# Strassen blocks of a gated up-projection: two taken together with interleaved products instead of one at a time, weight sums in buffers of their own, 19 activations kept in DRAM

## The chip, the core and the metric

The kernel runs on one core of a Trainium2 chip. The metric is the device time of one execution in microseconds, and the number to predict is the median of several executions of the changed kernel, against the median of the kernel before.

## The reference, cut to what matters

The whole program is one residual layer (a mixer and a feed-forward part). The change touches only the feed-forward part, which in numpy-like form is, for 512 tokens, model width D = 1024 and hidden width 2816:

```python
u, g = split(h @ w_ffn_up)             # h: 512 x 1024, w_ffn_up: 1024 x (2 x 2816)
g = causal_depthwise_conv3(g) + bias
act = gelu(g) * u                      # 512 x 2816
y = act @ w_ffn_down                   # 2816 x 1024, then scaled, residual, layer norm
```

All of it is fp32 in accuracy: each operand is held as a high part and a low part (fp32r), and a product is three matmuls (high x high, high x low, low x high).

## The kernel before

**Blocks.** The hidden width is cut into 22 blocks j of 128 columns. Each block has two units of weights of 128 x 1024: the gate unit 2j+1 and the value unit 2j. A plain block loads a unit (`wload`), casts it to its high part on ACT and subtracts on DVE for the low part (`wsplit`, L225 and L214), and runs 48 matmuls of 128 x 512 on PE (`up_mm`, lines L246 to L248). Its results stand in the PSUM tiles `acc` (gate, `gtile`) and `s` (value, `vtile`), two of each, taken by j mod 2. `gate_half` then copies, convolves (ACT L1203, then two DVE scalar_tensor_tensor, L206) and applies gelu (`gelu2`: ACT L566, DVE, ACT L568, DVE, a ping-pong between the two engines), and `val_half` multiplies by the value unit (DVE `tt`, L211).

**Fast blocks.** The blocks in `FAST` use Strassen's scheme (Winograd's form) on the 2 x 2 split of the two units and the tokens: seven products of 12 matmuls of 128 x 256 (`prod`, L1263) instead of eight. That needs four sums of weight halves on POOL (`gtt`, L349), each 128 x 512, and seven operand splits (`half`: an ACT cast L1226 and a DVE subtraction L214). The sums of the tokens (`x_combos`) are made once. In the order of its products, a fast block computes a (tile `hd`), copies a into b (`acc`, ACT L1283), computes c (`hd`) and copies it to SBUF (ACT L1286), adds a product to b, then forms d = b + c into `s` (DVE `tt`, L211) before b gets its next product. The sums are written over the halves they come from, in the `gab` tiles of the loaded units, so a sum waits for the split of the half that it overwrites. Six buffers hold split operands (`wh` and `wl` in turn, three of each).

**Order.** One block follows the other: 5, 7, 8, 10, 11, 13, 14, 16 and 17 are fast, the others plain; blocks 0 and 1 are computed ahead. Each engine's instructions run in the order in which a scheduler has put them, and the tile pools place the waits on buffers. After a block, `ada2_step` does parts of a modulation product on DVE (a scale of loaded weights, two scalar_tensor_tensor per part, tiles `s5h`), at the blocks listed in `MODS`. The first 8 activations (`NSP`) are written to DRAM and read back in the down-projection; the others are split at once and kept.

**Tail.** `tail_product` runs the down-projection over the 22 activations in the order `down`, three matmuls for each high and low pair, and prepares its weights (scale L211, cast L225, subtract L214) meanwhile.

Of the kernel before, what the change touches and what calls it, by code (L numbers as in the profile page):

```python
# [32 lines left out]
NF = 22  # L33
# [107 lines left out]
FAST = (5, 7, 8, 10, 11, 13, 14, 16, 17)  # L141
MODS = (6, 9, 12, 15, 18, 18, 19, 19)
NSP = 8
# [18 lines left out]
def _build(ctx, tc, nc, h):  # L162
# [1048 lines left out]
    def val_half(j, gg, ov):  # L1211
        if len(ov) == 1:
            tt(gg, ov[0], gg)
        else:
            for i in range(2):
                sl = slice(256 * i, 256 * i + 256)
                tt(gg[:, sl], ov[i][:, 0:256], gg[:, sl])
        if j < NSP:
            dma(spill[j * P:(j + 1) * P, :], gg)
            gp_.append(None)  # L1220
        else:
            gp_.append(pair_of(gg, "hb" if j < 14 else "s5b" if j < 15 else "hx" if j < 18 else "gab"))
# [7 lines left out]
    optag = iter(("wh", "wl") * (4 * NF))  # L1230
# [35 lines left out]
    def fast_pair(j):  # L1266
        wg_, wv_ = (wload(h["wup"][u], tag="gab") for u in (2 * j + 1, 2 * j))
        a11, a12, a21, a22 = wg_[:, :512], wg_[:, 512:], wv_[:, :512], wv_[:, 512:]
        b, d = gtile[j % 2], vtile[j % 2]
        a, c = bank("hd"), bank("hd")  # L1270
        w1 = half(a11)
        gtt(a21, a11, a21, ALU.subtract)
        s3 = half(a21)
        w4 = half(a22)
        gtt(a22, a22, a21, ALU.subtract)
        s2 = half(a22)
        w2 = half(a12)
        gtt(a11, a22, a11, ALU.add)
        s1 = half(a11)
        gtt(a12, a12, a22, ALU.subtract)  # L1280
        s4 = half(a12)
        prod(a, w1, xq(0, 0), True)
        A.copy(b[:, 0:256], a[:, 0:256])  # L1283
        prod(c, s3, xc(3), True)
        cs = hh(256)
        A.copy(cs, c[:, 0:256])  # L1286
        prod(b, s2, xc(2))
        tt(d[:, 0:256], b[:, 0:256], cs, ALU.add)
        prod(a, w2, xq(1, 0))
        prod(b, s1, xc(1))  # L1290
        v = hh(256)
        tt(v, b[:, 0:256], cs, ALU.add)
        prod(d, w4, xc(4))
        prod(b, s4, xq(1, 1))
        gg = gate_half(j, (a, b))
        val_half(j, gg, (d, v))
# [14 lines left out]
    for j in range(NF):  # L1311
        if j == G2J:
            g2 = grow(1, 0.5, "hd")
        if j >= FJ:
            first.append(scaled(h["wfd"][NSP + len(first)], g2, None))
        if j == NS // 2:
            x_combos()
        if j in FAST:
            fast_pair(j)
        else:  # L1320
# [23 lines left out]
    down = list(range(NSP, 18)) + list(range(NSP)) + list(range(18, NF))  # L1344
    got = {}

    def act_at(k):
        for kk in range(k, min(k + 3, NF)):
# [8 lines left out]
            got[kk] = pair_of(x, "s5h" if j < 4 else "hx" if j < 7 else "hb")  # L1357
# [20 lines left out]
```

## Time and profile before

| | |
|---|---|
| median of 3 runs (lowest, highest) | 897.4 us (896.97, 900.19) |
| the profiled execution | 899.05 us, span of its instructions 897.3 us |
| PE busy | 831.3 us, 93% of the span |
| DVE busy | 661.8 us, 74% |
| ACT busy | 389.7 us, 43% |
| POOL busy | 161.4 us, 18% |
| mean granted TensorE clock | 0.98 |

Busy shares are averages over a program with several stages. The change touches the stretch from 506.8 us, where the up-projection's block 2 begins, to the end. In the timeline rows below the first number is the start, the second the duration; several instructions that follow each other stand in one row with xN, and the bracket tells how long the engine was idle before and what released it.

### The profile page before, as it was taken

What the parts mean: (1) busy time and instruction counts of PE and PEld (TensorE: products, weight loads), DVE (VectorE), ACT (ScalarE), POOL (GpSimd) and SP (SyncE); (2) the same over time, 40 slices, a digit from 0 to 9 for tenths busy, and PEclk for the clock granted to TensorE, in tenths of its full rate; (3) what the DMA queues carried; (4) which work ended last, traced back from release to release, by engine and by line L of the source; (5) the groups of instructions that cost most, each with busy time, mean ns of one, the idle gap of its engine ahead of it and who ended that gap; (6) DMA issues with size and microseconds to landing.
All of it is one profiled execution on the core that took longest, in us unless ns stands there. A gap on an engine that the chain in (4) does not pass through costs nothing.

```text
span 897.3 us, 12212 instructions
## 1 busy us (share of the span) xinstructions
PE 831.3 (93%) x4430; PEld 685.5 (76%) x4430; DVE 661.8 (74%) x1232; ACT 389.7 (43%) x656; POOL 161.4 (18%) x285
## 2 busy tenths in 40 slices
PE   3999999999999999999999799977969799999996
PEld 1777878787777788888878688866868787888885
DVE  5557888788688855499888876868687688799044
ACT  4455464545656432333345544444445444345000
POOL 2771221112130000000024402414132200000000
PEclk9999999999999999999999899999889899999998
DMA  9832221312112344586550252332222053567011
GB/s 340 293 106 70 64 89 60 93 39 82 63 60 87 126 138 168 180 295 216 178 198 13 83 187 95 117 129 71 94 95 72 1 175 130 161 203 242 4 48 47
DMA packets 47725, 110.21 MB, mean 123 GB/s; under 512 B 13616, under 2 KB 14512, under 8 KB 47664
## 3 DMA queue, kind: packets, MB, share of 16 engines
q1 hardware_dynamic: 47664, 109.42, 36.9%
q8 instruction: 35, 0.57, 0.3%
q14 instruction: 26, 0.21, 0.1%
HBM read 103.11 MB, written 4.19 MB: 120 GB/s over the span
## 4 chain that ended last, share of the span: by engine, by line
PE 59%; DVE 21%; ACT 6%; DMA 4%; issue 4%; POOL 3%; SPq 2%; DVEq 0%; ACTq 0%; POOLq 0%
PE acc L246 8%; PE acc L248 8%; PE acc L247 8%; PE hd L246 6%; PE hd L247 6%; PE hd L248 6%; DVE hh L206 5%; DVE wl L214 3%; PE acc L1263 3%; POOL gab L349 3%; PE s L246 2%; PE s L248 2%; PE s L247 2%; SPq L196 2%; DVE wh L214 1%
## 5 line engine op out<-in xcount | busy, mean ns | idle before, releaser
L225 ACT CAST wh<-w 128x1024 fp32r<-128x1024 f32 (+2 forms) x85 | 84.5, 997 | 122.9 <-PE acc L247 73.2
L214 DVE TENSOR_TENSOR wl<-w,wh 128x1024 fp32r<-128x1024 f32 (+2 forms) x85 | 100.3, 1183 | 39.2 <-ACT wh L225 38.3
L246 PE MATMUL acc<-hp,wh 128*128 128x512 f32 x256 | 103.4, 405 | 0.4 <-ACT hx L789 0.4
L248 PE MATMUL acc<-hp,wl 128*128 128x512 f32 x256 | 102.0, 398 | 0.0
L247 PE MATMUL acc<-hp,wh 128*128 128x512 f32 x256 | 101.9, 398 | 0.0
L1028 POOL TENSOR_SCALAR mov<-mov 128x1 f32<-128x1 f32 x6 | 3.6, 608 | 326.6 <-ACT s L1027 160.2
L246 PEld LDWEIGHTS acc<-hp,wh 128*128 128x128 f32 x256 | 48.2, 189 | 14.7 <-issue 3.7
L248 PEld LDWEIGHTS acc<-hp,wl 128*128 128x128 f32 x256 | 48.2, 188 | 11.3 <-issue 0.4
L247 PEld LDWEIGHTS acc<-hp,wh 128*128 128x128 f32 x256 | 48.4, 189 | 10.8 <-issue 0.4
L349 POOL TENSOR_TENSOR gab<-gab,gab 128x512 f32<-128x512 f32 (+1 forms) x31 | 42.4, 1378 | 64.6 <-DMA gab<-in_wup 30.6
L206 DVE SCALAR_TENSOR_TENSOR s5h<-hh,k,s5h 128x512 f32<-128x512 f32 x56 | 41.7, 781 | 2.0 <-DMA hh<-in_wa 1.7
L1263 PE MATMUL acc<-hp,wl 128*128 128x256 f32 x120 | 21.5, 343 | 20.0 <-ACT acc L1283 19.8
L206 DVE SCALAR_TENSOR_TENSOR hh<-hd,hh 128x512 f32<-128x512 f32 (+3 forms) x40 | 24.4, 609 | 18.2 <-ACT hd L568 9.1
L1263 PEld LDWEIGHTS acc<-hp,wl 128*128 128x128 f32 x120 | 19.7, 248 | 21.0 <-ACT acc L1283 20.6
L214 DVE TENSOR_TENSOR wh<-gab,wh 128x512 fp32r<-128x512 f32 x32 | 26.5, 830 | 10.5 <-ACT wh L1226 10.5
L247 PE MATMUL hd<-s5b,wh 128*128 128x512 f32 (+1 forms) x88 | 32.2, 367 | 0.5 <-DVE s5b L214 0.5
L246 PE MATMUL hd<-s5b,wh 128*128 128x512 f32 (+1 forms) x88 | 31.8, 367 | 0.7 <-ACT s5b L1179 0.5
L225 ACT CAST hb<-hh 128x512 fp32r<-128x512 f32 (+3 forms) x44 | 24.7, 561 | 17.7 <-DVE hh L206 11.0
L248 PE MATMUL hd<-s5b,wl 128*128 128x512 f32 (+1 forms) x88 | 31.9, 364 | 0.0
L349 POOL TENSOR_TENSOR gab<-gab 128x512 f32<-128x512 f32 (+1 forms) x13 | 16.1, 1248 | 85.8 <-DVE wl L214 45.8
L1226 ACT CAST wh<-gab 128x512 fp32r<-128x512 f32 x32 | 19.4, 618 | 25.8 <-POOL gab L349 13.4
L214 DVE TENSOR_TENSOR wl<-gab,wl 128x512 fp32r<-128x512 f32 x31 | 28.5, 920 | 2.3 <-ACT wl L1226 1.5
(629 smaller groups left out, 2370.1 us busy)
## 6 DMA issues: line engine op xcount, KB each, us to landing
hh<-in_wa SPq DMA_DIRECT2D x64, 256.0 KB, 4.3
w<-in_win SPq DMA_DIRECT2D x30, 512.0 KB, 3.3
w<-in_wup SPq DMA_DIRECT2D x26, 512.0 KB, 3.4
w<-in_wfd SPq DMA_DIRECT2D x22, 512.0 KB, 3.7
gab<-in_wup SPq DMA_DIRECT2D x18, 512.0 KB, 3.4
hb<-in_wa SPq DMA_DIRECT2D x16, 512.0 KB, 7.3
w<-in_wglu SPq DMA_DIRECT2D x8, 512.0 KB, 3.4
w<-in_wdn SPq DMA_DIRECT2D x8, 512.0 KB, 3.3
```

The lines of the kernel that those rows point to most:

```text
L196: return nc.sync.dma_start(o, i)
L206: V.scalar_tensor_tensor(o, i0, s, i1, op0=op0, op1=op1)
L214: V.tensor_tensor(o, a, b, op=ALU.subtract)
L225: A.copy(hi, x)
L246: T.matmul(o, lhsT=wh, rhs=xh, start=first, stop=False)
L247: T.matmul(o, lhsT=wh, rhs=xl, start=False, stop=False)
L248: T.matmul(o, lhsT=wl, rhs=xh, start=False, stop=last)
L349: GP.tensor_tensor(o, a, b, op=op)
L1028: GP.tensor_scalar(v[:, 2:3], v[:, 0:1], v[:, 1:2], EPS * D, op0=ALU.add, op1=ALU.add)
L1226: A.copy(o[:, 0], src)
L1263: T.matmul(o[:, 0:256], lhsT=w[:, p, sl], rhs=x[k][y], start=first and k + i == 0, stop=k == 3 and i == 2, skip_group_check=True)
```

## The change

`FAST` now lists pairs: (5,6), (8,9), (11,12), (14,15) and (17,18), so ten blocks are fast and twelve plain. Between two pairs stands one plain block, and 19, 20 and 21 are plain at the end. `fast_pairs` emits the 14 products of a pair's blocks x and y in turns: a_x, c_x, a_y, c_y, b_x, a_x, b_y, a_y, b_x, d_x, b_y, d_y, b_x, b_y. The sums go into `hx` tiles of their own. Operands go to six `hb`, three `wh`, three `wl` and again two `hb` buffers. Two short buffers of a block become the halves of one `hh` tile. `x_combos` stands at block 4 in the source. Nineteen activations are written to DRAM and read back in the down-projection, which takes them in the order 0 to 21, and the parts of the modulation product are done at other blocks.

```diff
@@ -138,9 +138,10 @@
 MKR = 6
 PF = 1
 G2J = 20
-FAST = (5, 7, 8, 10, 11, 13, 14, 16, 17)
-MODS = (6, 9, 12, 15, 18, 18, 19, 19)
-NSP = 8
+FAST = (5, 8, 11, 14, 17)
+XJ = 4
+MODS = (7, 10, 10, 13, 13, 16, 16, 19)
+NSP = 19
 FJ = 21
 QUICK = (1, 3)
 LAST = ((0, 0, 512), (1, 0, 256), (1, 256, 512))
@@ -1219,7 +1220,7 @@
             dma(spill[j * P:(j + 1) * P, :], gg)
             gp_.append(None)
         else:
-            gp_.append(pair_of(gg, "hb" if j < 14 else "s5b" if j < 15 else "hx" if j < 18 else "gab"))
+            gp_.append(pair_of(gg, "gab"))
 
     def half(src):
         o = big((P, 2, 512), F32R, next(optag))
@@ -1227,7 +1228,7 @@
         sub(o[:, 1], src, f32(o[:, 0]))
         return o
 
-    optag = iter(("wh", "wl") * (4 * NF))
+    optag = iter((("hb",) * 6 + ("wh", "wl") * 3 + ("hb",) * 2) * NF)
     xd = []
 
     def x_combos():
@@ -1263,37 +1264,52 @@
                 T.matmul(o[:, 0:256], lhsT=w[:, p, sl], rhs=x[k][y], start=first and k + i == 0, stop=k == 3 and i == 2,
                          skip_group_check=True)
 
-    def fast_pair(j):
+    def fast_operands(j):
         wg_, wv_ = (wload(h["wup"][u], tag="gab") for u in (2 * j + 1, 2 * j))
         a11, a12, a21, a22 = wg_[:, :512], wg_[:, 512:], wv_[:, :512], wv_[:, 512:]
-        b, d = gtile[j % 2], vtile[j % 2]
-        a, c = bank("hd"), bank("hd")
-        w1 = half(a11)
-        gtt(a21, a11, a21, ALU.subtract)
-        s3 = half(a21)
-        w4 = half(a22)
-        gtt(a22, a22, a21, ALU.subtract)
-        s2 = half(a22)
-        w2 = half(a12)
-        gtt(a11, a22, a11, ALU.add)
-        s1 = half(a11)
-        gtt(a12, a12, a22, ALU.subtract)
-        s4 = half(a12)
-        prod(a, w1, xq(0, 0), True)
-        A.copy(b[:, 0:256], a[:, 0:256])
-        prod(c, s3, xc(3), True)
-        cs = hh(256)
-        A.copy(cs, c[:, 0:256])
-        prod(b, s2, xc(2))
-        tt(d[:, 0:256], b[:, 0:256], cs, ALU.add)
-        prod(a, w2, xq(1, 0))
-        prod(b, s1, xc(1))
-        v = hh(256)
-        tt(v, b[:, 0:256], cs, ALU.add)
-        prod(d, w4, xc(4))
-        prod(b, s4, xq(1, 1))
-        gg = gate_half(j, (a, b))
-        val_half(j, gg, (d, v))
+        r3, r2, r1, r4 = (hx() for _ in range(4))
+        gtt(r3, a11, a21, ALU.subtract)
+        gtt(r2, a22, r3, ALU.subtract)
+        gtt(r1, r2, a11, ALU.add)
+        gtt(r4, a12, r2, ALU.subtract)
+        return a11, r3, r2, a12, r1, a22, r4
+
+    def fast_pairs(js):
+        src = [fast_operands(j) for j in js]
+        a, c, b, d, cv = {}, {}, {}, {}, {}
+        for j in js:
+            b[j], d[j] = gtile[j % 2], vtile[j % 2]
+
+        def op(i, n):
+            return half(src[i][n])
+
+        def first(i, j):
+            a[j], c[j] = bank("hd"), bank("hd")
+            cv[j] = hh()
+            prod(a[j], op(i, 0), xq(0, 0), True)
+            A.copy(b[j][:, 0:256], a[j][:, 0:256])
+            prod(c[j], op(i, 1), xc(3), True)
+            A.copy(cv[j][:, 0:256], c[j][:, 0:256])
+
+        def second(i, j):
+            prod(b[j], op(i, 2), xc(2))
+            tt(d[j][:, 0:256], b[j][:, 0:256], cv[j][:, 0:256], ALU.add)
+            prod(a[j], op(i, 3), xq(1, 0))
+
+        def third(i, j):
+            prod(b[j], op(i, 4), xc(1))
+            tt(cv[j][:, 256:512], b[j][:, 0:256], cv[j][:, 0:256], ALU.add)
+            prod(d[j], op(i, 5), xc(4))
+
+        def fourth(i, j):
+            prod(b[j], op(i, 6), xq(1, 1))
+
+        for part in (first, second, third, fourth):
+            for i, j in enumerate(js):
+                part(i, j)
+        for j in js:
+            gg = gate_half(j, (a[j], b[j]))
+            val_half(j, gg, (d[j], cv[j][:, 256:512]))
 
     early = [(u, wsplit(h["wup"][u], tags=("wh", "wl") if i < 3 else ("hb", "hb")), bank("hd"))
              for i, u in enumerate((1, 0, 3, 2)[:NS])]
@@ -1312,12 +1328,12 @@
         if j == G2J:
             g2 = grow(1, 0.5, "hd")
         if j >= FJ:
-            first.append(scaled(h["wfd"][NSP + len(first)], g2, None))
-        if j == NS // 2:
+            first.append(scaled(h["wfd"][len(first)], g2, None))
+        if j == XJ:
             x_combos()
         if j in FAST:
-            fast_pair(j)
-        else:
+            fast_pairs((j, j + 1))
+        elif j - 1 not in FAST:
             ou = {}
             for u in (2 * j + 1, 2 * j):
                 if u in pre:
@@ -1341,7 +1357,7 @@
         for n in range(2):
             dma(h["out"][t * P:(t + 1) * P, n * 512:(n + 1) * 512], r[n])
         yield
-    down = list(range(NSP, 18)) + list(range(NSP)) + list(range(18, NF))
+    down = list(range(NF))
     got = {}
 
     def act_at(k):
@@ -1354,7 +1370,7 @@
                 continue
             x = hh()
             dma(x, spill[j * P:(j + 1) * P, :])
-            got[kk] = pair_of(x, "s5h" if j < 4 else "hx" if j < 7 else "hb")
+            got[kk] = pair_of(x, "hx" if j % 7 < 3 else "s5h")
         return got[k]
 
     tail_product(act_at, [h["wfd"][j] for j in down], g2, "hh", NF, 8, [("s5b", "s5b")] * 2 + [("hp", "hp")] * 4 + [("hb", "hb")] * 2, finish2, FDB, first)
```

Line numbers of the kernel after are one higher for the helpers (L215 for L214, L212 for L211, L207 for L206, L227 for L226); the copy of a into b is L1290 for L1283.

On DVE, before, this stands around the place where fast block 10 forms d (the seventh row; `s5_1058` is a tile `s`). Ahead of it are the multiplication of plain block 9 (`hh_1198`), one part of the modulation (two instructions on `s5h`) and splits.

```order
L214 TENSOR_TENSOR wl_1214_6052<-gab_1206_6032,wl_1214_6052 128x512
L211 TENSOR_TENSOR hh_1198_5986<-s5_1059_4898,hh_1198_5986 128x512
L206 SCALAR_TENSOR_TENSOR s5h_1155_5668<-hh_1204_6026,k_15_92,s5h_1155_5668 128x512
L214 TENSOR_TENSOR hb_1203_6023<-hh_1198_5986,hb_1203_6023 128x512
L206 SCALAR_TENSOR_TENSOR s5h_1156_5669<-hh_1205_6029,k_15_92,s5h_1156_5669 128x512
L214 TENSOR_TENSOR wl_1216_6060<-gab_1206_6032,wl_1216_6060 128x512
L211 TENSOR_TENSOR s5_1058_4897<-acc_1056_4895,hh_1217_6088 128x256
L214 TENSOR_TENSOR wh_1228_6177<-gab_1224_6171,wh_1228_6177 128x512
L214 TENSOR_TENSOR wl_1229_6181<-gab_1225_6173,wl_1229_6181 128x512
L214 TENSOR_TENSOR wh_1230_6184<-gab_1225_6173,wh_1230_6184 128x512
L211 TENSOR_TENSOR hh_1218_6127<-acc_1056_4895,hh_1217_6088 128x256
```

And now, where block 11 of the pair (11,12) forms d (the last row), behind the end of plain block 10's gelu, with `hb_1265` and `hb_1266` the last operands of this pair, and `hb_1303` and `hb_1304` the first operands of the next one:

```order
L207 SCALAR_TENSOR_TENSOR hd_1227_6134<-hd_1227_6134,hh_1225_6129 128x512
L207 SCALAR_TENSOR_TENSOR hh_1226_6133<-hd_1227_6134,hh_1225_6129 128x512
L212 TENSOR_TENSOR hh_1226_6133<-s5_1058_4897,hh_1226_6133 128x512
L215 TENSOR_TENSOR hb_1265_6401<-hx_1240_6190,hb_1265_6401 128x512
L215 TENSOR_TENSOR hb_1266_6416<-hx_1246_6202,hb_1266_6416 128x512
L207 SCALAR_TENSOR_TENSOR s5h_1178_5811<-hh_1231_6171,k_15_92,s5h_1178_5811 128x512
L215 TENSOR_TENSOR hb_1303_6574<-gab_1288_6547,hb_1303_6574 128x512
L207 SCALAR_TENSOR_TENSOR s5h_1179_5812<-hh_1232_6174,k_15_92,s5h_1179_5812 128x512
L215 TENSOR_TENSOR hb_1304_6590<-hx_1290_6551,hb_1304_6590 128x512
L207 SCALAR_TENSOR_TENSOR s5h_1178_5811<-hh_1233_6177,k_15_92,s5h_1178_5811 128x512
L207 SCALAR_TENSOR_TENSOR s5h_1179_5812<-hh_1234_6180,k_15_92,s5h_1179_5812 128x512
L212 TENSOR_TENSOR s5_1059_4898<-acc_1057_4896,hh_1249_6209 128x256
```

The step d = b + c now stands behind two splits of the pair's last operands, two parts of the modulation (four instructions) and two splits for the next pair; the two gelus of the earlier pair and that of the plain block stand ahead of those.

On ACT, before, at the second of two fast blocks, block 11 (its copy of a into b is the last but one row; `gab_1224` and `gab_1225` are its own units with their sums, and `hd_1222` the gelu of fast block 10):

```order
L1202 COPY hh_1220_6154<-hd_1208_6036 128x256
L1226 CAST wl_1231_6188<-gab_1225_6173 128x512
L1202 COPY hh_1220_6154<-acc_1056_4895 128x256
L1226 CAST wl_1233_6195<-gab_1224_6171 128x512
L1203 ACTIVATE hh_1219_6153<-hh_1220_6154,k_1_63 128x512
L566 ACTIVATE hd_1222_6161<-hh_1219_6153 128x512
L568 ACTIVATE hd_1222_6161<-hd_1222_6161 128x512
L1226 CAST wh_1234_6199<-gab_1224_6171 128x512
L1283 COPY acc_1057_4896<-hd_1226_6175 128x256
L1286 COPY hh_1235_6227<-hd_1227_6176 128x256
```

Now, at the start of the pair (11,12) (`hd_1247` and `hd_1252` are a of block 11 and of block 12, `hd_1227` the gelu of plain block 10):

```order
L567 ACTIVATE hd_1227_6134<-hh_1225_6129 128x512
L569 ACTIVATE hd_1227_6134<-hd_1227_6134 128x512
L1290 COPY acc_1057_4896<-hd_1247_6207 128x256
L1227 CAST hb_1265_6401<-hx_1240_6190 128x512
L1227 CAST hb_1266_6416<-hx_1246_6202 128x512
L1290 COPY acc_1056_4895<-hd_1252_6242 128x256
L1227 CAST hb_1303_6574<-gab_1288_6547 128x512
L1292 COPY hh_1249_6209<-hd_1248_6208 128x256
L1292 COPY hh_1254_6244<-hd_1253_6243 128x256
L1227 CAST hb_1304_6590<-hx_1290_6551 128x512
```

Block 12's copy of a into b no longer stands behind a gelu of block 11; both copies stand behind the gelu of the plain block ahead of the pair, and only casts of sums made a period earlier are between them.

On ACT, before, where the up-projection ends (`gab` is the split of activation 21, `wh` of down weights):

```order
L225 CAST wh_1409_7415<-hh_1411_7417 128x512
L225 CAST wh_1409_7415<-hh_1412_7421 128x512
L225 CAST gab_1399_7378<-hh_1394_7341 128x512
L225 CAST wh_1414_7451<-hh_1416_7453 128x512
L225 CAST wh_1414_7451<-hh_1417_7457 128x512
L225 CAST wh_1419_7487<-hh_1421_7489 128x512
```

And now:

```order
L567 ACTIVATE hd_1419_7412<-hh_1417_7407 128x512
L569 ACTIVATE hd_1419_7412<-hd_1419_7412 128x512
L226 CAST gab_1423_7448<-hh_1418_7411 128x512
L226 CAST hx_1433_7461<-hh_1432_7459 128x512
L226 CAST wh_1442_7503<-hh_1444_7505 128x512
L226 CAST hx_1436_7467<-hh_1435_7465 128x512
```

Behind the cast of activation 21 stands `hx_1433`, the cast of activation 0 read back from DRAM, with which the first matmul of the down-projection now works; before it worked with a kept activation in `hb`.

## Rows read from the trace of the kernel before

**Rows 1.** Stages: us, busy (x instructions) of PE, PEld, DVE, ACT, POOL, clock, DMA.

```profile
547.66:558.00 10.34, 10.07 (x85) 9.86 (x84) 5.32 (x9) 5.18 (x10) 2.26 (x2) 1.00 0.48 150
638.24:679.02 40.78, 33.88 (x218) 31.04 (x217) 30.71 (x43) 20.03 (x37) 11.79 (x8) 0.92 0.27 91
719.10:763.80 44.70, 43.90 (x188) 34.79 (x187) 37.03 (x52) 19.39 (x28) 0.00 (x0) 1.00 0.46 153
```

**Rows 2.** Waits of PE, 480 to 740 us: total us, times, longest.

```profile
PE acc L1263 <- ACT acc L1283: 20.3, 5, 5.3
PE acc L1263 <- DVE s L211: 5.9, 5, 1.6
PE acc L246 <- ACT wh L225: 2.7, 1, 2.7
```

**Rows 3.** Timeline of PE, 638 to 680: start, us, instruction [idle <-releaser].

```profile
638.24 0.39 PE L246 MATMUL acc<-s5b,wh 128*128 128x512 f32 x1
...
649.38 1.58 PE L1263 MATMUL hd<-s5b,wl 128*128 128x256 f32 x12
...
661.29 1.58 PE L1263 MATMUL hd<-s5b,wh 128*128 128x256 f32 x12
662.70 1.52 PE L1263 MATMUL hd<-hp,wl 128*128 128x256 f32 x12
669.52 2.93 PE L1263 MATMUL acc<-hp,wl 128*128 128x256 f32 x12 [5.30 <-ACT acc L1283]
...
679.02 0.39 PE L246 MATMUL acc<-s5b,wh 128*128 128x512 f32 x1
```

**Rows 4.** Timeline of ACT, 662 to 671 us.

```profile
669.09 0.38 ACT L1283 COPY acc<-hd 128x256 f32<-128x256 f32 x1
```

**Rows 5.** Timeline of DVE, 656 to 671 us.

```profile
658.11 0.68 DVE L214 TENSOR_TENSOR wh<-gab,wh 128x512 fp32r<-128x512 f32 x1
...
659.37 1.40 DVE L214 TENSOR_TENSOR wh<-gab,wh 128x512 fp32r<-128x512 f32 x1 [0.23 <-ACT wh L1226]
660.91 3.26 DVE L214 TENSOR_TENSOR wl<-gab,wl 128x512 fp32r<-128x512 f32 x2
664.10 2.53 DVE L206 SCALAR_TENSOR_TENSOR hh<-hh,k,hh 128x510 f32<-128x510 f32 x2
667.36 0.70 DVE L206 SCALAR_TENSOR_TENSOR hd<-hd,hh 128x512 f32<-128x512 f32 x1 [0.73 <-ACT hd L566]
668.70 0.69 DVE L206 SCALAR_TENSOR_TENSOR hh<-hd,hh 128x512 f32<-128x512 f32 x1 [0.65 <-ACT hd L568]
...
670.24 0.42 DVE L211 TENSOR_TENSOR hh<-hh,hh 128x256 f32<-128x256 f32 x1
```

**Rows 6.** Timeline of POOL, the same stretch.

```profile
658.93 1.30 POOL L349 TENSOR_TENSOR gab<-gab 128x512 f32<-128x512 f32 x1 [4.70 <-DVE wh L214]
660.30 4.99 POOL L349 TENSOR_TENSOR gab<-gab,gab 128x512 f32<-128x512 f32 x3
```

**Rows 7.** Clock by stretch (PEclk after POOL's column).

```profile
512.35:517.20 4.85, 4.85 (x11) 3.80 (x12) 3.47 (x5) 1.59 (x3) 1.28 (x1) 0.50 0.95 339
...
669.50:672.25 2.75, 2.73 (x13) 2.73 (x13) 1.16 (x3) 0.89 (x2) 0.00 (x0) 0.50 0.39 127
...
674.20:677.00 2.80, 2.80 (x25) 2.80 (x25) 1.12 (x1) 1.32 (x2) 0.52 (x1) 0.98 0.00 0
```

**Rows 8.** DVE groups by form, 638.24 to 679.02: busy us, mean ns.

```profile
L214 DVE TENSOR_TENSOR wl<-gab,wl 128x512 fp32r<-128x512 f32 x7 | 6.5, 932 | 0.3
L214 DVE TENSOR_TENSOR wh<-gab,wh 128x512 fp32r<-128x512 f32 x7 | 6.0, 861 | 1.4 <-ACT wh L1226 1.4
```

**Rows 9.** Timeline of DVE late in the down-projection.

```profile
850.33 0.69 DVE L208 SCALAR_TENSOR_TENSOR hh<-hx,acc 128x512 f32<-128x512 f32 x1 [18.87 <-PE acc L248]
```

**Rows 10.** Timeline of PE and ACT where the down-projection starts.

```profile
767.11 0.40 PE L246 MATMUL acc<-wh,hb 128*128 128x512 f32 x1
...
768.46 0.62 ACT L225 CAST gab<-hh 128x512 fp32r<-128x512 f32 x1
```

## The prediction

> **What bounds the kernel now.** I read the page first: PE is busy 93% of the span, so time can come only from matmuls saved or from holes in PE. The stage table shows where the holes are [rows 1]. Fast block 5 takes 10.34 us, nearly all of it PE. The stretch of plain block 12 with fast blocks 13 and 14 takes 40.78 us with PE busy for 33.88, the granted clock at 0.92. The late plain blocks have PE at 43.90 of 44.70 us. So the fast blocks that follow each other are the only part of the up-projection with much idle time on PE.
>
> The list of PE's waits names it [rows 2]. Two waits come back in every such stretch: about 5.3 us for the ACT copy of a into b, and 1.6 us for the DVE sum d. PE's timeline places the first [rows 3]: the plain block runs from 638.24 to 649.38 (11.14 us), the second fast block starts at 661.29, does two products (1.41 us from start to start) and then stands for 5.30 us. The copy that it waits for starts at 669.09 [rows 4], 6.2 us after the end of its product at 662.87 [rows 3]. On ACT it stands behind the gelu of the block before, and that gelu was late on DVE: two splits took 3.26 us together and two convolution steps 2.53 [rows 5], while POOL did sums [rows 6]. After the hole the clock is 0.50 from 669.50 to 674.20 and 0.98 after it [rows 7]; the first product then takes 2.93 us [rows 3]. At half speed those 4.7 us hold 2.35 us of work: the hole costs 5.3 and then 2.3 more.
>
> **The terms of the sum.** Dense, a product is 1.41 us, a pair's 14 are 19.8, and plain block and pair together 31.0 (a *period*). The change makes ten fast blocks of nine: a plain block becomes fast, 11.14 against 9.9, 1.2 us less. The rest is what becomes of the holes, four periods of about 40.8 before.
>
> *Removed.* The copy no longer waits for a gelu of its neighbour, which has moved a plain block ahead: the 5.3 us wait in that form goes. Sums are no longer behind splits of their own block.
>
> *Added: a chain through DVE.* Count from the end of a pair's 13th product. DVE must then do the gelus of both blocks and of the plain block in its order, then the last splits of the next pair and the modulation, and only then d for its block x; product 9 (b of x again) waits for that. One gelu, undisturbed: two ACT copies and the first convolution part about 1.4, two DVE steps 1.4, then from the end of the second step (666.63) to the last multiplication (670.66) 4.0 less a split of 0.6 in between [rows 5]: 6.2 us. The second and third have their ACT part behind them: 4.8 each. So 15.8; three splits that stand between convolution steps, at 0.6, make 17.6 (three others fall into the ping-pong's waits of 0.73 and 0.65 [rows 5]). Behind them are four splits (2.4) and four modulation steps (2.7), and d itself 0.4: 23.1, to which small waits add 0.2. Products 9 to 13 are 7.1: 30.4 us, just under the 31.0 of a dense period. In the first period (plain 7) the modulation is four scalar_tensor_tensor shorter: 27.7.
>
> *POOL's sums on that chain.* Each of the first three periods holds the eight sums for the pair after next, in buffers of their own, at places where DVE runs that chain. What a sum costs DVE: alone a split is 0.68 us [rows 5]; in the stretch from 659.37 the three splits and two steps took 1.40 + 3.26 + 2.53 = 7.2 [rows 5] against 0.68 + 1.28 + 1.4 alone, so 3.8 more for four sums [rows 6], 0.95 each. As a mean over the whole stretch the 14 splits took 861 and 932 ns [rows 8], 3.0 us more for eight sums, 0.38 each. At most a sum costs all of its 1.30 us [rows 6]. I take 0.95, since on the chain DVE has always something to do, as it had in that stretch: 7.6 us a period, bounds 3.0 and 10.4.
>
> The Trainium skill (SBUF — State Buffer, section "Who interferes with whom") says that a DVE instruction with two SBUF inputs and a GpSimd instruction that reads SBUF share one port pair as an exclusive lock, so that the loser waits altogether. By that each sum would cost its full duration, the upper bound here, and the sum below would be 895. The trace bears the direction out, and shows 0.95 of 1.30.
>
> *The clock.* With 7.6 us more the chain ends after the dense period, and the wait ahead of product 9 is some 3 to 4 us (the rest of the delay falls on products 3 to 5, which wait for the gelus). A hole of 5.3 us was followed by 0.50, and the head's hole of 2.7 us [rows 2] with a second one by 0.50 too [rows 7]; so I add the same 2.3 us. Below: nothing. Above: five products at 2.93 [rows 3], 1.52 more each, 7.6.
>
> *Periods.* First: 27.7 + 7.6 + 2.3 = 37.6. Second and third: 30.4 + 9.9 = 40.3. The fourth (plain 16, pair 17, 18) has no sums left: 31.0 + 0.3. Together 149.5.
>
> *Sums in buffers of their own, twelve operand buffers, loads.* These cost no instruction; a fast block has the same two loads. Nothing, while the DMA share is 0.27 in such a stretch [rows 1]; a load that came late would delay POOL, not PE, since sums are a period ahead.
>
> *x_combos at block 4.* On the engines the instructions still stand ahead of block 2's weights: the head's wait [rows 2] stays. Nothing.
>
> *Activations in DRAM.* Eleven more are written and read back. Eleven casts and splits leave the up-projection and join the down-projection, where DVE finished the weights so early that it then stood idle for 18.87 us until 850.33 [rows 9]; 11 x 0.6 = 6.6 us of DVE fits, spread over the steps. Nothing; without that cover it would cost up to 6.6. But the first step of the down-projection, at 767.11 now with no wait [rows 10], needs activation 0, whose cast stands on ACT behind the one of activation 21. That one waits for the last matmul and the multiplication (0.68), and a cast is 0.62 [rows 10]: 0.68 + 2 x 0.62, with two handovers 2.1 us on the path. Bounds: 0 (if activation 0 arrives and is cast by then) and 3.
>
> *The sum.* Block 5 begins at 547.66 [rows 1], its pair's 13th product ends 18.4 later, at 566.05. With 149.5 for the periods, 1.4 for the 14th product and 36.9 for plain 19 to 21 (719.10 [rows 1] to 767.11 [rows 10] less 11.14) the up-projection ends at 753.85, 13.3 earlier than 767.11. With 2.1 back: 11.2 us. The profiled execution took 899.05 us, so it would be 887.9; the median of before is 897.4, and the forecast is **886 us**.
>
> **The rivals.**
>
> *A lighter chain.* If sums cost the mean of 0.38 and the clock stays up, the periods are 31.0, 33.4, 33.4 and 31.3, 20.4 less: 866. For it: before, the holes for d were 1.6 us at most, with sums in the same stretch [rows 2]. Against it: sums and chain fall together. With all periods dense it would be 861.
>
> *The wait only changes its name.* DVE does about 30.7 us of work in such a stretch of 40.78 [rows 1], and the same splits, gelus and sums remain; if every period, the last one too, stays at 40.8, they are 13.7 longer: 900, no change. For it: three gelus now run in series ahead of d. Against it: the last period has no sums.
>
> *The clock, and slower.* The holes now lie ahead of product 9 with five products of the chain behind it. If the clock stays at half for all five, each of three periods is 5.3 longer: 902, and with sums at 1.30 it is 910. The point from which it decides is 6.0 us of clock loss a period (four of the five products at half clock): there it equals before. For it: 2.93 us in a product after the hole. Against it: before, the clock came back within two products [rows 7].
>
> **How the numbers follow.** Chances: the forecast case 0.50 (its own range 880 to 895, the upper bound of the lock at the top), the lighter chain 0.20, dense 0.05, the wait that changes its name 0.13, the clock 0.12. A measurement of this kernel can tell about 0.5% from no change, so "the same" is 892.9 to 901.9. Faster: all of the first three but a small end of the forecast case, 0.70. Same: most of the changed name, half of the clock case, that end: 0.19. Slower: the rest, 0.11. For eight in ten the range goes from the lighter chain to the changed name: 864 to 901.
>
> **What would show it.** PE's waits should show no 5.3 us on the copy (L1290) twice over but a wait of product matmuls on DVE's d (L212) of 3 to 4 us in three periods, beside waits for gelus (L207) at products 3 to 5; periods of about 38, 40, 40 and 31; splits (L215) beside sums at 1.3 to 1.7 us; the clock at 0.50 behind the holes; one new wait of 2 us for the cast of activation 0 and none later. The prediction is wrong if splits beside sums stay near 0.7, if d comes early and another engine holds PE, or if the fourth period is as long as the second.

## The result, and the profile after

The kernel after takes 886.16 us, the median of 4 runs (883.47 to 890.18); the kernel before, timed beside it, 897.67 (896.97 to 900.19). The ratio is 0.987, 95% interval 0.9828 to 0.9913: faster by 11.5 us, where 11.2 were forecast. The runs of this kernel scatter more than those of before, and between the two profiled executions, on which the forecast's sum was made, the gain is 13.5 us (899.05 to 885.54): that the medians agree to 0.3 us is luck.

The stage table of the kernel after, cut at the start of each pair's 14th product (columns as in [rows 1]), shows the four periods that the forecast was made of:

```profile
565.63:603.11 37.48, 33.27 (x218) 30.42 (x217) 31.76 (x40) 17.95 (x33) 12.48 (x8) 0.95 0.37 125
603.11:642.25 39.14, 33.38 (x218) 30.30 (x217) 33.93 (x42) 17.95 (x33) 12.59 (x8) 0.96 0.38 125
642.25:680.56 38.31, 33.28 (x218) 30.43 (x217) 32.54 (x42) 17.95 (x33) 12.79 (x8) 0.96 0.40 132
680.56:712.51 31.95, 31.51 (x218) 28.87 (x217) 23.28 (x37) 15.71 (x28) 0.00 (x0) 1.00 0.28 94
```

37.5, 39.1, 38.3 and 32.0 us, 146.9 together, where 37.6, 40.3, 40.3 and 31.3, 149.5, were forecast. The last one has no POOL in it (0.00), the clock at 1.00 and PE nearly full; the first three are 5.5 to 7.2 us longer.

The waits of PE from 480 to 883 us (total, times, longest):

```profile
PE hd L1264 <- DVE hh L207: 12.5, 6, 3.8
...
PE acc L1264 <- DVE s L212: 3.0, 2, 1.5
```

The 5.3 us on the copy of a into b [rows 2] are gone. The longest wait is now one on L207, the end of a gelu, and the wait for d (L212) is short. PE's timeline shows where they lie:

```profile
587.34 1.99 PE L1264 MATMUL hd<-hp,hb 128*128 128x256 f32 x12 [3.80 <-DVE hh L207]
589.12 2.76 PE L1264 MATMUL acc<-hp,hb 128*128 128x256 f32 x12
...
596.05 1.57 PE L1264 MATMUL acc<-hp,wh 128*128 128x256 f32 x12
...
624.94 2.05 PE L1264 MATMUL hd<-hp,hb 128*128 128x256 f32 x12 [3.80 <-DVE hh L207]
...
635.27 1.65 PE L1264 MATMUL acc<-hp,wh 128*128 128x256 f32 x12 [1.44 <-DVE s L212]
```

587.34 is product 4, c of block y. It needs an hd bank, and the bank is free when the plain block's gelu is done. DVE's timeline shows that gelu's last step at 586.59, and why it is so late:

```profile
572.97 1.77 DVE L207 SCALAR_TENSOR_TENSOR hh<-hh,k,hh 128x510 f32<-128x510 f32 x1
574.67 1.78 DVE L215 TENSOR_TENSOR wh<-hx,wh 128x512 fp32r<-128x512 f32 x1
576.37 1.78 DVE L207 SCALAR_TENSOR_TENSOR hh<-hh,k,hh 128x511 f32<-128x511 f32 x1
578.08 1.78 DVE L215 TENSOR_TENSOR wl<-gab,wl 128x512 fp32r<-128x512 f32 x1
...
586.59 0.69 DVE L207 SCALAR_TENSOR_TENSOR hh<-hd,hh 128x512 f32<-128x512 f32 x1 [0.65 <-ACT hd L569]
...
594.34 0.42 DVE L212 TENSOR_TENSOR s<-acc,hh 128x256 f32<-128x256 f32 x1
...
634.80 0.42 DVE L212 TENSOR_TENSOR s<-acc,hh 128x256 f32<-128x256 f32 x1
```

The four instructions from 572.97 take 1.77 us each, where steps of the kind took 0.7. On POOL, sums of a later pair fill the same stretch (first and last of four):

```profile
572.64 1.56 POOL L350 TENSOR_TENSOR hx<-gab,gab 128x512 f32<-128x512 f32 x1 [10.31 <-DMA gab<-in_wup]
...
577.57 1.74 POOL L350 TENSOR_TENSOR hx<-gab,hx 128x512 f32<-128x512 f32 x1
```

Behind the hole of 3.80 us the clock falls within product 4 (0.82 on average), is at half in product 5 and back with product 6 (clock in the column behind POOL's):

```profile
587.34:589.20 1.86, 1.86 (x13) 1.86 (x14) 1.86 (x3) 1.63 (x5) 0.50 (x1) 0.82 1.00 358
589.20:591.70 2.50, 2.50 (x14) 2.50 (x14) 2.23 (x3) 0.89 (x2) 2.42 (x2) 0.50 0.34 124
591.70:594.00 2.30, 2.30 (x20) 2.30 (x20) 2.30 (x3) 1.21 (x3) 1.75 (x2) 0.95 0.00 0
```

Products 4 to 6 take 5.9 us from 587.34 to 593.22 instead of 4.2. In the first period nothing else waits: product 9 starts at 596.05 with no wait, d having been formed from 594.34 to 594.76. In the second, d is formed from 634.80, and product 9 waits 1.44 us for it; in the third it waits 1.55 us. Last, the start of the down-projection:

```profile
750.61 0.39 PE L249 MATMUL s<-hx,wl 128*128 128x512 f32 x1
752.95 0.50 PE L247 MATMUL acc<-wh,hx 128*128 128x512 f32 x1 [1.95 <-ACT hx L226]
```

It waits 1.95 us for the cast of activation 0, where 2.1 was forecast [rows 10].

### The profile page after: what moved, and what is told of

The parts are those of the page before. It is cut to its first block, busy times and chain, and to the rows that moved or that the text cites. A ratio compares the mean times of both kernels' runs of the same rounds, so it can differ in the third digit from the quotient of the medians.

```text
span 883.8 us, 12383 instructions
## 1 busy us (share of the span) xinstructions
PE 826.0 (93%) x4466; PEld 682.2 (77%) x4466; DVE 675.0 (76%) x1240; ACT 391.8 (44%) x665; POOL 173.7 (20%) x289
## 4 chain that ended last, share of the span: by engine, by line
PE 64%; DVE 21%; ACT 6%; issue 4%; DMA 3%; SPq 2%; POOL 1%; DVEq 0%; ACTq 0%; POOLq 0%
PE acc L247 8%; PE acc L249 8%; PE acc L248 8%; PE hd L247 6%; DVE hh L207 6%; PE hd L248 6%; PE hd L249 6%; PE acc L1264 4%; PE hd L1264 3%; PE s L247 2%; PE s L248 2%; PE s L249 2%; PE s L1264 2%; SPq L197 2%; DVE wl L215 1%
## 5 line engine op out<-in xcount | busy, mean ns | idle before, releaser
L226 ACT CAST wh<-w 128x1024 fp32r<-128x1024 f32 (+2 forms) x83 | 82.4, 995 | 109.7 <-PE acc L248 64.8
L215 DVE TENSOR_TENSOR wl<-w,wh 128x1024 fp32r<-128x1024 f32 (+2 forms) x83 | 99.0, 1195 | 21.9 <-ACT wh L226 19.1
L249 PEld LDWEIGHTS acc<-hp,wl 128*128 128x128 f32 x256 | 48.2, 188 | 11.2 <-issue 0.4
L207 DVE SCALAR_TENSOR_TENSOR s5h<-hh,k,s5h 128x512 f32<-128x512 f32 x56 | 44.9, 842 | 5.9 <-DMA hh<-in_wa 5.9
L207 DVE SCALAR_TENSOR_TENSOR hh<-hd,hh 128x512 f32<-128x512 f32 (+3 forms) x40 | 24.4, 609 | 21.0 <-ACT hd L569 12.3
L350 POOL TENSOR_TENSOR hx<-gab,gab 128x512 f32<-128x512 f32 x10 | 15.1, 1508 | 99.6 <-DMA gab<-in_wup 90.1
L350 POOL TENSOR_TENSOR hx<-gab,hx 128x512 f32<-128x512 f32 x20 | 32.6, 1632 | 4.8 <-DVE hb L215 3.4
L247 PE MATMUL hd<-s5b,wh 128*128 128x512 f32 (+1 forms) x88 | 31.8, 367 | 0.7 <-ACT s5b L1180 0.5
L249 PE MATMUL hd<-s5b,wl 128*128 128x512 f32 (+1 forms) x88 | 31.9, 363 | 0.0
L567 ACT ACTIVATE hd<-hh 128x512 f32<-128x512 f32 x22 | 13.2, 601 | 40.9 <-DVE hh L207 40.8
L248 PE MATMUL acc<-hx,wh 128*128 128x512 f32 x74 | 29.2, 394 | 0.0
L247 PE MATMUL acc<-hx,wh 128*128 128x512 f32 x74 | 29.1, 394 | 0.0
L249 PE MATMUL acc<-hx,wl 128*128 128x512 f32 x74 | 29.1, 393 | 0.0
L1264 PE MATMUL hd<-hp,hb 128*128 128x256 f32 x120 | 17.7, 300 | 11.5 <-DVE hh L207 11.5
L212 DVE TENSOR_TENSOR hh<-w,hh 128x512 f32<-128x512 f32 x42 | 27.3, 685 | 1.1 <-DMA w<-in_wfd 1.1
```

Of the source, the lines that this page charges most:

```text
L207: V.scalar_tensor_tensor(o, i0, s, i1, op0=op0, op1=op1)
L212: V.tensor_tensor(o, a, b, op=op)
L215: V.tensor_tensor(o, a, b, op=ALU.subtract)
L226: A.copy(hi, x)
L247: T.matmul(o, lhsT=wh, rhs=xh, start=first, stop=False)
L248: T.matmul(o, lhsT=wh, rhs=xl, start=False, stop=False)
```

## The experiments

**The sums left out.** Is it POOL's sums that hold DVE's chain?

```diff
-        r3, r2, r1, r4 = (hx() for _ in range(4))
-        gtt(r3, a11, a21, ALU.subtract)
...
-        return a11, r3, r2, a12, r1, a22, r4
+        return a11, a21, a22, a12, a11, a22, a12
```

> The kernel after without POOL's weight sums: the four operands that are sums are split from the loaded halves themselves (so the output is another). Everything else stays. If the sums beside the DVE chain cost the three long periods (37.5, 39.1, 38.3 us from one pair's 13th product to the next's), these come down to the 32.0 us of the period without sums, the holes of 3.5 to 3.8 us ahead of the second product of block y go, the clock stays at 1.00, and the time is about 867. Rival: the three gelus in series and the hd banks hold that product whatever POOL does; then the holes stay above 2.5 us and the time is 880 or more.

Measured: 869.95 us (868.55 to 870.9), ratio to before 0.9686 (0.9671 to 0.97), 16 us under the kernel after and 3 us over the 867 that were expected. The waits of PE on the two:

```profile
PE acc L1264 <- DVE s L212: 3.1, 2, 1.9
...
PE hd L1264 <- DVE hh L207: 1.6, 4, 0.4
```

The holes of 3.5 to 3.8 us are holes of 0.4, four of them, so the bank and the three gelus in series alone hold product 4 by 0.4 us. What one instruction costs with and without sums is seen in the DVE groups by form. The kernel after, 566 to 680 us:

```profile
L207 DVE SCALAR_TENSOR_TENSOR s5h<-hh,k,s5h 128x512 f32<-128x512 f32 x8 | 11.2, 1424 | 0.7 <-DMA hh<-in_wa 0.7
...
L215 DVE TENSOR_TENSOR wl<-gab,wl 128x512 fp32r<-128x512 f32 x9 | 9.5, 1050 | 2.0 <-ACT wl L1227 2.0
```

The same without sums:

```profile
L215 DVE TENSOR_TENSOR wl<-gab,wl 128x512 fp32r<-128x512 f32 x11 | 7.5, 686 | 1.8 <-ACT wl L1227 1.8
...
L207 DVE SCALAR_TENSOR_TENSOR s5h<-hh,k,s5h 128x512 f32<-128x512 f32 x8 | 6.0, 751 | 5.0 <-DMA hh<-in_wa 5.0
```

A step of the modulation takes 1424 ns instead of 751 and a split 1050 instead of 686. The same difference over all the groups of DVE that grew is some 23 us for the 24 sums of the stretch: just under 1.0 us a sum, where the prediction took 0.95. A sum itself takes 1.5 to 1.6 us on POOL there. A gelu step with one input in PSUM (`hd`) does not grow; in the kernel after, one lies wholly beside a sum (in the run with the sums twice five do, at 0.69 us each):

```profile
654.88 1.74 POOL L350 TENSOR_TENSOR hx<-gab,hx 128x512 f32<-128x512 f32 x1
...
655.39 0.69 DVE L207 SCALAR_TENSOR_TENSOR hd<-hd,hh 128x512 f32<-128x512 f32 x1
```

The rule of the Trainium skill (SBUF — State Buffer, "Who interferes with whom"), by which a DVE instruction with two SBUF inputs and a GpSimd instruction that reads SBUF contend for an exclusive lock, is borne out in its direction, and so is what it says of a DVE instruction with at most one SBUF input (it does not contend, outside the two-port modes); that a sum costs DVE all of its duration is not, on average.

Without sums the four periods are 31.9, 33.2, 33.8 and 32.0 us between 14th products, and the second and third still have a wait for d, 1.9 us at most. DVE's timeline of the second, whose 14th product starts at 595.80 (the end of the plain block's gelu, the last step of the modulation, d):

```profile
612.71 0.69 DVE L207 SCALAR_TENSOR_TENSOR hh<-hd,hh 128x512 f32<-128x512 f32 x1 [0.65 <-ACT hd L569]
...
620.87 0.75 DVE L207 SCALAR_TENSOR_TENSOR s5h<-hh,k,s5h 128x512 f32<-128x512 f32 x1 [0.92 <-DMA hh<-in_wa]
621.54 0.43 DVE L212 TENSOR_TENSOR s<-acc,hh 128x256 f32<-128x256 f32 x1
```

The three gelus end 17.6 us after the start of the 14th product, where the kernel after has 21.8 (603.11 to 624.89), and d ends after 26.2 us, where it has 32.1. Of the 26.2, DVE stands 2.2 us for loads of the modulation's operands, in the third period 2.8 of 26.8; the chain alone is 24.0 us in both. So on the chain the eight sums cost 7.9 and 6.6 us, 0.8 to 1.0 each, and part of what their absence saves is taken up by loads that the sums had hidden.

**The sums made twice.** Each `gtt` line is doubled.

```diff
         gtt(r3, a11, a21, ALU.subtract)
+        gtt(r3, a11, a21, ALU.subtract)
...
```

> The kernel after with each weight sum made twice on POOL, the second time over the same result. If a sum costs DVE's chain about 1 us, eight more sums a period make the three long periods some 5 to 9 us longer: 900 to 912. Rival: sums run beside DVE at little cost, POOL is busy for only a third of a period; then under 890.

Measured: 905.7 us (903.94 to 907.46), ratio to before 1.0087 (1.0066 to 1.0109), 19.5 over the kernel after. Taking the sums away gave 16, doubling them cost 20, but not in the same places: the three long periods are 40.7, 40.8 and 44.1 us, 3.2, 1.7 and 5.8 more (5 to 9 were expected), and 7.3 us were lost ahead of the first of them, where the sums of the first pairs stand. In one pair PE's timeline now has the hole ahead of product 9 that the prediction had expected of the kernel after, and the half clock behind it:

```profile
646.08 2.93 PE L1264 MATMUL acc<-hp,wh 128*128 128x256 f32 x12 [5.91 <-DVE s L212]
...
677.50 2.93 PE L1264 MATMUL hd<-hp,hb 128*128 128x256 f32 x12 [4.26 <-DVE hh L207]
```

The first row is product 9 of the pair (11,12), the second product 4 of the next pair.

**The sums on DVE.**

```diff
-        gtt(r3, a11, a21, ALU.subtract)
+        tt(r3, a11, a21, ALU.subtract)
...
```

> The kernel after with the weight sums on DVE instead of POOL. By the theory of the lock a sum costs the chain about 1.0 us on POOL and 0.6 us on DVE, so the three long periods are some 3 us shorter each and the time is 874 to 880. Rival: DVE is the bound by its sum of work, or stands in order behind loads that are not there; then 886 to 895.

Measured: 871.64 us (871.05 to 872.68), ratio 0.9707 (0.9692 to 0.9721). The direction was right, the size too small: 14.5 us instead of 6 to 12. On DVE a sum is one more instruction, 0.69 us long and 0.6 from start to start:

```profile
L212 DVE TENSOR_TENSOR hx<-gab,hx 128x512 f32<-128x512 f32 x12 | 8.2, 686 | 0.0
```

On POOL it costs DVE 0.8 to 1.0 and takes 1.5 to 1.6 itself. The periods are 33.5, 33.4, 34.3 and 31.9: no wait of PE there is longer than 1.5 us, and the granted clock of the run is 0.993, of the kernel after 0.987.

**One block after the other.**

```diff
-        for part in (first, second, third, fourth):
-            for i, j in enumerate(js):
+        for i, j in enumerate(js):
+            for part in (first, second, third, fourth):
                 part(i, j)
```

> The kernel after with the products of a pair one block after the other (x's seven, then y's seven); sums, buffers and gelus as in the kernel after. Product 5 then waits for d of block x, which comes at 29 to 32 us of a period, and nine products follow it instead of five: periods about 4 to 5.6 us longer, the time 900 to 906. Rival: the interleaving is worth nothing, and sums in buffers of their own did it: 884 to 890.

Measured: 869.78 us (869.25 to 871.86), ratio 0.9689 (0.9674 to 0.9704). Both theories were wrong: without the interleaving the kernel is 16 us faster. PE's timeline of the run (the last product of the pair (8,9); then product 5 of block x and the last product of the pair (11,12), which wait):

```profile
598.10 1.33 PE L1264 MATMUL acc<-s5h,hb 128*128 128x256 f32 x9
...
618.60 1.70 PE L1264 MATMUL acc<-hp,hb 128*128 128x256 f32 x12 [0.61 <-DVE s L212]
...
632.36 1.34 PE L1264 MATMUL acc<-s5h,hb 128*128 128x256 f32 x9 [1.42 <-DVE hh L212]
```

And DVE's:

```profile
598.56 0.69 DVE L207 SCALAR_TENSOR_TENSOR hd<-hd,hh 128x512 f32<-128x512 f32 x1
...
599.90 0.69 DVE L207 SCALAR_TENSOR_TENSOR hh<-hd,hh 128x512 f32<-128x512 f32 x1
...
618.12 0.43 DVE L212 TENSOR_TENSOR s<-acc,hh 128x256 f32<-128x256 f32 x1
```

Block x's seven products end in the middle of the pair, so x's gelu runs while y's products do: the step at 599.90 is the end of x's gelu, and the pair's last product begins at 598.10. The chain after the pair is two gelus instead of three. It also has four sums beside it instead of eight, as POOL's timeline shows (the first of the four, and the next after them):

```profile
605.38 1.29 POOL L350 TENSOR_TENSOR hx<-gab,gab 128x512 f32<-128x512 f32 x1 [11.28 <-DMA gab<-in_wup]
...
622.61 1.69 POOL L350 TENSOR_TENSOR hx<-gab,gab 128x512 f32<-128x512 f32 x1 [11.06 <-DMA gab<-in_wup]
```

From the start of the 14th product to the start of d of the next pair it is now 20.0 us (598.10 to 618.12), in the kernel after 31.7 (603.11 to 634.80). d is needed four products earlier, and yet the wait for it is 0.61 us. The expectation had kept the chain of the interleaved kernel, with its three gelus and the sums where they were, and only moved the place where d is needed.

**The activations and the modulation alone**, in the kernel before: `MODS`, `NSP = 19`, `down` and the tags of the split activations as in the kernel after.

```diff
-MODS = (6, 9, 12, 15, 18, 18, 19, 19)
-NSP = 8
+MODS = (7, 10, 10, 13, 13, 16, 16, 19)
+NSP = 19
...
-    down = list(range(NSP, 18)) + list(range(NSP)) + list(range(18, NF))
+    down = list(range(NF))
```

> The kernel before with only the activations and the modulation as in the kernel after (19 activations in DRAM, order 0 to 21, the parts of the modulation at the other blocks). By the theory these gain little: one split and one cast less in each block's chain, some 1 us a stretch of three blocks, against 2 us at the start of the down-projection: 892 to 898. Rival: the splits moved into the down-projection are the gain of the change; then 884 to 889.

Measured: 898.88 us (894.73 to 901.29), ratio 0.9999 (0.9982 to 1.0016), a little above the range. By themselves, in the kernel before, these are worth nothing.

**Ten fast blocks alone**, in the kernel before.

```diff
-FAST = (5, 7, 8, 10, 11, 13, 14, 16, 17)
+FAST = (5, 6, 8, 9, 11, 12, 14, 15, 17, 18)
```

> The kernel before with ten fast blocks, at the same places as in the kernel after (5, 6, 8, 9, 11, 12, 14, 15, 17, 18), but one after the other, with sums in place and six operand buffers. Each plain block with two fast ones keeps its 40 us and the first two fast blocks get the wait of 5.3 us and the clock's 2.3: 900 to 904. Rival: one fast block more is worth its 1.2 us or more, or the placement is the gain: 885 to 896.

Measured: 906.1 us (905.37 to 907.93), ratio 1.0091 (1.0072 to 1.0109), some 2 us above the range. One more fast block, with two side by side five times instead of four, makes that kernel slower; its waits on the copy are eight instead of five [rows 2]:

```profile
PE acc L1263 <- ACT acc L1283: 25.5, 8, 5.0
```

**Twelve operand buffers, sums in place.** The kernel before with its activations in DRAM and the modulation moved (as two experiments above), ten fast blocks one after the other, and

```diff
-    optag = iter(("wh", "wl") * (4 * NF))
+    optag = iter((("hb",) * 6 + ("wh", "wl") * 3 + ("hb",) * 2) * NF)
```

> Ten fast blocks one after the other, twelve operand buffers, activations in DRAM, but POOL's sums in place in the loaded units as in the kernel before. If sums in buffers of their own are what let a block's operands be ready a block ahead, this keeps the wait of 5 us on the copy of a into b: 895 to 905. Rival: the operand buffers did it; then 868 to 880.

Measured: 893.43 us (890.64 to 897.22), ratio 0.9948 (0.9932 to 0.9964), a little under the range. The wait on the copy did not stay, as the expectation had it: it fell to 3.7 us in all. Others took its place:

```profile
PE acc L246 <- ACT wh L225: 10.7, 5, 4.0
PE acc L1263 <- DVE s L211: 9.6, 5, 2.9
PE acc L1263 <- ACT acc L1283: 3.7, 4, 1.1
```

The time says that the operand buffers bring a third of the way from 906 to 870. The waits say that the expectation's reason was wrong: it is the operand buffers that end most of the wait on the copy, and PE now stands for weights of plain blocks (L225) and for d.

**Sums in buffers of their own, six operand buffers**, in the version with one block after the other.

```diff
-    optag = iter((("hb",) * 6 + ("wh", "wl") * 3 + ("hb",) * 2) * NF)
+    optag = iter(("wh", "wl") * (7 * NF))
```

> The version with the products one block after the other and sums in buffers of their own, with the six operand buffers of the kernel before. If the sums' buffers are the part that pays, most of the gain stays: 872 to 885. Rival: six buffers, shared with the plain block's weights, keep the operands as late as before: 895 or more.

Measured: 875.21 us (875.01 to 877.96), ratio 0.9752 (0.9734 to 0.9771). So of the way from 906 to 870, sums of their own (with both blocks' sums made ahead of the pair, which goes with it) bring most with either number of buffers: 893.4 to 869.8 with twelve, 906.1 to 875.2 with six (there with the activations moved as well). Twelve instead of six are worth 5.4 us once the sums have their own.

**Gelu's scratch tile in SBUF**, in the kernel after.

```diff
-        gelu2(gg, a, lambda: bank("hd"))
+        gelu2(gg, a, hh)
```

> The kernel after with gelu's scratch tile in SBUF instead of an hd bank. Product 4 then no longer waits for the plain block's gelu (3.5 to 3.8 us in three periods). By the theory that DVE's chain is the bound, the hole moves to product 9, which waits for d longer (3 to 6 us), and the time is 884 to 890. Rival: the bank alone was the bound; then the periods lose the 3.8 us and the clock's 2 us each: 868 to 874.

Measured: 884.69 us (882.43 to 888.3), ratio 0.9854 (0.9825 to 0.9884); the kernel after has 0.987 (0.9828 to 0.9913). No wait for a gelu is left in front of product 4. The holes stand ahead of product 9 in the second and third period, with the half clock behind them (in the first the longest is 1.84 us, ahead of product 11):

```profile
633.63 2.93 PE L1264 MATMUL acc<-hp,wh 128*128 128x256 f32 x12 [5.79 <-DVE s L212]
...
672.67 2.93 PE L1264 MATMUL acc<-hp,wh 128*128 128x256 f32 x12 [4.70 <-DVE s L212]
```

So the bank only says where the hole is; DVE's chain says how long it is.

**The hole filled with work of no use**, in the kernel after.

```diff
-            prod(a[j], op(i, 0), xq(0, 0), True)
+            w0 = op(i, 0)
+            prod(a[j], w0, xq(0, 0), True)
...
+            if i:
+                for _ in range(2):
+                    prod(d[js[0]], w0, xq(0, 0), True)
             prod(c[j], op(i, 1), xc(3), True)
```

> The kernel after with two products more ahead of product 4, written to the bank of d of block x before it is used (work of no use, 2.8 us inside the hole of 3.8). Products 4 and 5 should take 1.4 to 1.6 us instead of up to 2.8, the clock stay over 0.95; the first period gains 2 us, the second and third under 1, since d is their bound: 880 to 885. Rival: the clock falls whatever stands in the hole, and the time is that of the kernel after or up to 8 us more.

Measured: 893.65 us (892.28 to 893.91), ratio 0.9946 (0.9929 to 0.9962). The time is that of the rival, but the run does not answer its question: the scheduler put 20 of the 24 matmuls ahead of the pair, where they wait for d's bank, so the hole lies ahead of them and not around them. PE's timeline and the clock of that stretch:

```profile
583.05 4.15 PE L1264 MATMUL s<-s5b,hb 128*128 128x256 f32 x20 [3.48 <-DVE hh L212]
```

```profile
583.00:587.00 4.00, 3.95 (x20) 3.95 (x21) 3.55 (x6) 1.42 (x4) 0.00 (x0) 0.58 0.27 92
```

20 matmuls of 128 x 256, dense 2.4 us, took 4.0 (583.05 to 587.04). The clock falls behind a hole of 3.5 us here too; whether matmuls inside the hole would have kept it up was not shown.

**Together: one block after the other, sums on DVE.** Both edits above.

> The version with the blocks' products one after the other, and its sums on DVE. Its holes that are left (0.3 to 1.9 us) lie behind DVE instructions that run beside sums; without the lock the four periods are 32 to 32.9 us and the time is 863 to 866. Rival: sums in DVE's own row delay gelus and d as much as the lock did: 869 or more.

Measured: 862.34 us (861.78 to 864.35), ratio 0.9603 (0.9587 to 0.9618), a little under the range. Periods of 31.1, 32.1, 31.8 and 31.8. The waits of PE from 540 us to the end of the matmuls:

```profile
PE acc L247 <- ACT hx L226: 2.0, 1, 2.0
PE acc L1264 <- DVE s L212: 0.9, 2, 0.5
PE acc L1264 <- DVE hh L212: 0.8, 2, 0.6
```

Little is left but the start of the down-projection. **With activation 19 first there:**

```diff
-    down = list(range(NF))
+    down = [19] + list(range(19)) + [20, 21]
...
-            first.append(scaled(h["wfd"][len(first)], g2, None))
+            first.append(scaled(h["wfd"][19 if not first else len(first) - 1], g2, None))
```

> The same with activation 19, which is kept, first in the down-projection. The 2.0 us wait for the cast of activation 0 goes: 2 us below the run without it. Rival: the wait goes to the next step (activation 0 is still cast late) and the time is the same.

Measured: 861.06 us (859.19 to 865.25), ratio 0.9591 (0.9561 to 0.962). The 2.0 us row is gone from the waits and nothing came in its place, but the intervals of the two versions overlap, so in the time it is not shown. Either version is faster than both kernels, 4% under the kernel before.

## Why the prediction was right

*The bound of the kernel before* was read rightly: holes in the fast blocks, through gelus and splits late on DVE beside sums. *One fast block more is worth 1.2 us*: only where the holes go with it; in the kernel before it cost 7.5.

*The chain and the price of a sum.* d was forecast to end 23.3 + 7.6 = 30.9 us after the 13th product; counted from the start of the 14th it ended after 32.1 us in the second period and 31.1 in the third. The two parts hold by themselves: 24.0 for the chain without sums, 6.6 to 7.9 for eight sums. This term carries the forecast, and the runs show it from both sides: without sums the three periods are 5.6, 5.9 and 4.5 us shorter, with twice as many 3.2, 1.7 and 5.8 longer. Without sums the periods shrink by less than the sums cost the chain, since the modulation's loads then hold d; why twice as many lengthen them by less than twice is open.

*The place of the hole* is the step that failed. I had 3 to 4 us ahead of product 9 and the rest at products 3 to 5. It was the other way round: 3.5 to 3.8 us ahead of product 4 and at most 1.55 ahead of product 9. I had named the wait for the gelu, and given it too little, though my own terms give it, with half of the eight sums beside the gelus: 17.6 us and four times 0.95 make 21.4, and product 4 would begin, dense, at 1.4 + 11.14 + 3 x 1.41 = 16.8. The gelu's end was measured at 21.7, 21.8 and 20.6 us, and at 17.6 without sums. In the second and third period the place makes no difference to the time, since d comes after it. In the first it does: d ended after 29.1 us, where product 9 could have begun, and began after 30.4, held by the hole at product 4 and the clock behind it. That the period came to 37.5 us for 37.6 is luck.

*The clock* was counted in all three long periods at 2.3 us. It was lost in all three, about 1.6 us, but at products 4 to 6. In the second and third period product 9 then waited for d anyway, and DVE waited for nothing of PE's ahead of d, so by these rows it cost nothing there; in the first 1.3 us lay on the path. With the clock taken out of those two periods, the forecast of 40.3 becomes 38.0, against 39.1 and 38.3 measured. These 4.6 us less, and 2.0 that the four periods ran over, are where the 149.5 and the 146.9 part.

*Terms at nothing* stood: activations and modulation, measured alone, gave a ratio of 0.9999. The cover in the down-projection held: behind its first matmul no wait of PE is listed. Two waits that the prediction had not, 1.29 and 0.67 us for the weights of block 21 (738.59 and 739.99), stand ahead of it; the last three blocks still took 37.1 us for 36.9. *The start of the down-projection*: 1.95 for 2.1.

*What the prediction did not ask* is what the interleaving is worth. It credited it with the end of the 5.3 us wait, since the neighbour's gelu moves a plain block ahead, and charged the three gelus in series to the whole change. The runs part the two: with the products one block after the other that wait is gone as well (0.2 us in all on L1290), so twelve operand buffers and sums of their own, made ahead for both blocks, end it, and the interleaving has only the price. In steps: 898.6 us before, 906.1 with ten fast blocks, 893.4 with twelve operand buffers (and the activations moved), 869.8 with sums of their own (and `x_combos` at block 4), 886.2 interleaved. The price of the last step depends on the sums: 16.4 us with them on POOL, where eight instead of four lie on the chain, and 9.3 with them on DVE (862.3 to 871.6).

Of the rivals, the lighter chain fell with the 0.8 to 1.0 us a sum, the one of the clock with its return with product 6, and the wait that only changes its name with the fourth period.

## What to carry to other kernels

When products of two blocks are interleaved to hide a dependence, look at what starts when a block ends: here both blocks' gelus were put off to the end of the pair, on the engine that was already late. Work on GpSimd beside a chain of VectorE instructions with two SBUF inputs is not free: price it by those instructions beside it and alone, and try it on VectorE itself if it is shorter there. And, by these rows, a lower clock costs only as much as a later wait does not take up.

## What the runs showed of the hardware

Moving work from GpSimd to the busier VectorE made the kernel 14.5 us faster: a 128 x 512 sum takes 0.69 us there and 1.3 to 1.8 on GpSimd. Beside sums VectorE's tensor_scalar grew too (`s5h<-hh,k`, L201: 484 ns without sums, 1352 with them, two of each).

Matmul holes of 3.5 to 3.8 us were followed by half clock, which cost the three products behind them some 1.65 us; behind one of 5.3 half clock lasted longer, from 669.50 to 674.20 [rows 7]. Holes of 1.44 and 1.55 us were not: the granted clock is 1.00 from 635.27 to 638.00 and from 673.38 to 676.00. Near 1.9 us the runs show both: in the version with one block after the other 1.88 us ahead of 666.65 were followed by 0.60 and then 0.50 until 670.40, in the run without sums 1.85 us ahead of 655.85 were followed by 1.00.
